# Strassen-type up projection: part sums on VectorE, the MLP's output turned row block by row block, and the gate's norm gain folded into its weights

## The chip, the cores and the metric

The kernel runs on one core of a Trainium2 chip. The metric is the device time of one execution in microseconds (us); less is better. Engines are named as the profile names them: PE is TensorE, DVE is VectorE, ACT is ScalarE, POOL is GpSimd, SP issues the weight loads.

## What is computed

One layer of a hybrid decoder for 512 tokens and a width of 1024, everything in float32. Before the stretch that the change touches lie the input projections, a gated linear recurrence, stick-breaking attention and their merge `m`. The change touches what follows:

```
x = x + merged @ w_out
h2 = rmsnorm(x, norm_mlp_g)
x = x + square(relu(h2 @ w_mlp_up)) @ w_mlp_down      # 1024 -> 4096 -> 1024
h3 = rmsnorm(x, norm_ple_g)
x = x + sigmoid(h3 @ w_ple_gate) * (p @ w_ple)
return rmsnorm(x, norm_final_g)
```

## The kernel before

**Precision and weights.** PE multiplies in fp32r. Each float32 operand is split in a high part, rounded to fp32r by a cast on ACT (L55), and a low part, the difference, formed on DVE (L56); `split_scaled` (L59, L60) does the same for an operand that is to be multiplied by a gain per partition. `prod` (L119 to L124) makes every product of three matmuls: high by high, high by low, low by high. Weights come in halves of 128 partitions by 1024 columns (512 KB): SP loads one into a `raw` buffer (3 of them), ACT and DVE split it into `whi` and `wlo` (3 each). `next_half` hands out the half whose turn it is in the list `halves`, and has the next one loaded and split. The instructions of each engine are put in order by a scheduler at build time, and each engine runs its own list in that order; buffers are given by pools and tags, and a tile that takes the space of an older one waits until that is read out.

**Up projection.** The weight of a group `g` (of 8) consists of four quarters, rows r and columns c. In place of eight products of quarters, seven are made (L623, L625, L626), numbered 1 to 7. Their activations are sums of halves of `x1`, made once during the output projection and kept split in `xa`, `xb`, `xc` (L587 to L604). Their weights are quarters (1: quarter 00, 2: 10, 3: 11) or sums of quarters: 5 is 01 - 00, 7 is 11 - 01, 6 is 11 less the sum of 5, 4 is 10 less the sum of 6. `up_part` (a maker that `next_half` calls) forms a sum in `tw` on POOL (L570) and splits it. `tw` has tag F1, the space of `x1`, which the last additions on DVE (L595, L604) still read. A product is 24 matmuls of 256 columns, a group 168. The order in a group is UP_ORDER, (1, 7, 5, 6, 3, 2, 4). The results are put together in `u` and `w`: u is product 1 plus 6, w is 7 plus 5, then w + u on POOL (L652); `relu2` makes the activation of the next projection on ACT (L634, L635).

**Between.** Blocks of `x1` are turned into rows `x1t` (`to_rows`) as they come. The squares for the norm (`sqm`) follow at once. After the last group, `p` is split into `psp`, whose space is that of `xa`; the small product `p @ w_ple` gives `ple`.

**Down projection.** 32 steps of 24 matmuls of 512 columns go into eight PSUM banks `dn`, in DN_ORDER; each step splits its activation into `ah`, `al` (pool `dnx`) and its weight half. The last three steps go row block by row block, and after each block DVE adds the scaled bank to `x2t` (L716).

**Tail.** When all blocks are through, `x2t` is turned by PE (L725, eight tiles x2T of four 128 by 128 transposes), multiplied by the gain of the norm on DVE (L727, `xg`) and split into `h3` (L728). The gate's weight halves pg0 to pg2 are in the stream of halves; pg3 to pg7 are loaded into `wb3` and `wb1`. The gate product `pgt` runs for all row blocks over the first six of eight parts, then over the last two, then `gate_post`.

Of the kernel before, what the change touches and what calls it, by code (L numbers as in the profile page):

```python
# [27 lines left out]
UP_ORDER = (1, 7, 5, 6, 3, 2, 4)  # L28
DN_ORDER = [h + 2 * g + i for g in range(8) for h in (0, 16) for i in range(2)]
# [5 lines left out]
def hybrid_layer(ctx, tc, xT, pT, vecs, gfin, gates, w_in, w_bl, w_ba, w_out,  # L35
# [202 lines left out]
    with tc.tile_pool(name="st", bufs=1) as st, \  # L238
# [304 lines left out]
    sums = []  # L543
    raws = {}

    def quarter(g, r, c):
# [4 lines left out]
    def up_part(gi, name, kt):

        g, i = gi
        if i == 1:
            src = quarter(g, 0, 0)
        elif i == 2:
            src = quarter(g, 1, 0)
        elif i == 3:
            src = quarter(g, 1, 1)
        else:  # L560
            if not sums:
                sums.append(big.tile([P, 4, 1024], F32, tag="F1", name="tw"))
            tw = sums[0]
            src = tw[:, i - 4]
            a, b = {7: ((1, 1), (0, 1)), 5: ((0, 1), (0, 0)), 6: ((1, 1), None), 4: ((1, 0), None)}[i]
            b = quarter(g, *b) if b else tw[:, 1] if i == 6 else tw[:, 2]
# [8 lines left out]
    makers["up"] = up_part  # L575
    for n in OUT_ORDER:
# [22 lines left out]
        to_rows(x1, x1t, n)  # L599

    ssm = const.tile([P, 2 * NB], F32, name="ssm")
    for tb in range(NB):
        for h in range(2):
            t = tmp_tile(f"sqm{tb}{h}")  # L604
            sc.activation(t, x1t[:, tb, h * 512:(h + 1) * 512], AF.Square,
                          accum_out=ssm[:, 2 * tb + h:2 * tb + h + 1])
    rs2 = const.tile([P, NB], F32, name="rs2")
    ssv = ssm.rearrange("p (t h) -> p t h", h=2)
    ve.tensor_tensor(rs2, ssv[:, :, 0], ssv[:, :, 1], op=ALU.add)
    ve.tensor_scalar(rs2, rs2, 1.0 / D, EPS, op0=ALU.mult, op1=ALU.add)  # L610
    ve.reciprocal(rs2, rs2)


    act = [big.tile([P, 16, 2, H], F32, tag="B1", name="act0"), big2.tile([P, 16, 2, H], F32, tag="B3", name="act1")]
# [20 lines left out]

    for g in range(8):
# [8 lines left out]
        sc.copy(w, by)
        bz = bank(pp, f"upZ{g}")
        products(g, 5, bz, True)
        ve.tensor_tensor(w, bz, w, op=ALU.add)
# [223 lines left out]
```

## Time and profile before

| what | us |
|---|---|
| median of 3 runs | 958.0 |
| the runs | 952.49 to 958.74 |
| the profiled execution | 956.24 |
| its span in the trace | 954.5 |
| PE busy | 923.2 |
| DVE busy | 619.7 |
| ACT busy | 503.3 |
| POOL busy | 174.9 |

The profiled execution lies 1.8 us below the median; 1.7 us of it lie outside its span. A row of the trace that gives one instruction reads: start and duration in us, engine, line, operation, output and inputs, shapes, number of instructions; in brackets, how long the engine had waited and which instruction released it. Durations of matmuls are modelled and overlap; a matmul's cost is read from start to start.

### The profile page before, as it was taken

What the parts mean: (1) busy time and instruction counts of PE and PEld (TensorE: products, weight loads), DVE (VectorE), ACT (ScalarE), POOL (GpSimd) and SP (SyncE); (2) the same over time, 40 slices, a digit from 0 to 9 for tenths busy, and PEclk for the clock granted to TensorE, in tenths of its full rate; (3) what the DMA queues carried; (4) which work ended last, traced back from release to release, by engine and by line L of the source; (5) the groups of instructions that cost most, each with busy time, mean ns of one, the idle gap of its engine ahead of it and who ended that gap; (6) DMA issues with size and microseconds to landing.
All of it is one profiled execution on the core that took longest, in us unless ns stands there. A gap on an engine that the chain in (4) does not pass through costs nothing. (4 is left out here: it accounts for less than half of the span.)

```text
span 954.5 us, 12767 instructions
## 1 busy us (share of the span) xinstructions
PE 923.2 (97%) x4858; PEld 793.9 (83%) x4858; DVE 619.7 (65%) x851; ACT 503.3 (53%) x794; POOL 174.9 (18%) x187
## 2 busy tenths in 40 slices
PE   8989999999999999999999699999999999999896
PEld 7878888888888888888888699999988888888685
DVE  6697766889998985435566677677753333332866
ACT  6455868767777764422244556656554323222633
POOL 0010000133242330000000466666500000000000
PEclk9999999999999999999999799999999999999999
DMA  7232232321212212522321233332243223233302
GB/s 240 93 110 89 67 107 69 111 67 67 67 67 67 67 67 67 198 89 89 111 88 45 76 102 91 114 106 90 89 133 109 90 93 106 89 103 118 111 0 89
DMA packets 25116, 89.46 MB, mean 94 GB/s; under 512 B 2912, under 2 KB 2912, under 8 KB 24800
## 3 DMA queue, kind: packets, MB, share of 16 engines
q1 hardware_dynamic: 24480, 87.61, 28.2%
q10 hardware_dynamic: 576, 1.05, 0.3%
q8 instruction: 38, 0.62, 0.3%
q14 instruction: 22, 0.18, 0.1%
HBM read 86.55 MB, written 2.10 MB: 93 GB/s over the span
## 5 line engine op out<-in xcount | busy, mean ns | idle before, releaser
L123 PE MATMUL dn<-wlo_dn,ah 128*128 128x512 f32 x256 | 99.7, 390 | 0.0
L124 PE MATMUL dn<-whi_dn,al 128*128 128x512 f32 x256 | 98.8, 389 | 0.0
L122 PE MATMUL dn<-whi_dn,ah 128*128 128x512 f32 x256 | 98.0, 390 | 0.0
L56 DVE TENSOR_TENSOR wlo_up<-tw,whi_up 128x1024 fp32r<-128x1024 f32 x32 | 73.0, 2300 | 29.8 <-ACT whi_up L55 29.8
L570 POOL TENSOR_TENSOR tw<-raw_up,raw_up 128x1024 f32<-128x1024 f32 x16 | 45.4, 2840 | 219.5 <-DVE s L595 167.4
L56 DVE TENSOR_TENSOR al<-act,ah 128x512 fp32r<-128x512 f32 x32 | 21.9, 692 | 87.7 <-ACT ah L55 87.7
L55 ACT CAST ah<-act 128x512 fp32r<-128x512 f32 x32 | 19.7, 624 | 104.6 <-PE dn L123 104.6
L160 POOL TENSOR_SCALAR_AFFINE_SELECT r<-r 128x128 f32<-128x128 f32 x64 | 29.9, 467 | 179.1 <-ACT r L428 174.5
L432 DVE TENSOR_TENSOR_SCAN pr<-r,zero 128x128 f32<-128x128 f32 (+1 forms) x64 | 54.2, 847 | 10.6 <-POOL r L160 10.1
L123 PEld LDWEIGHTS dn<-wlo_dn,ah 128*128 128x128 f32 x256 | 48.3, 189 | 10.2
L122 PEld LDWEIGHTS dn<-whi_dn,ah 128*128 128x128 f32 x256 | 48.3, 189 | 10.0
L124 PEld LDWEIGHTS dn<-whi_dn,al 128*128 128x128 f32 x256 | 48.0, 188 | 10.0
L56 DVE TENSOR_TENSOR wlo_dn<-raw_dn,whi_dn 128x1024 fp32r<-128x1024 f32 x32 | 39.2, 1225 | 24.3 <-ACT whi_dn L55 24.3
L570 POOL TENSOR_TENSOR tw<-raw_up,tw 128x1024 f32<-128x1024 f32 x16 | 45.0, 2814 | 2.4 <-DMA raw_up<-in_w_up_dram 1.8
L623 PE MATMUL upY<-xa,whi_up 128*128 128x256 f32 x128 | 37.4, 292 | 6.7 <-ACT whi_up L55 6.7
L55 ACT CAST whi_up<-tw 128x1024 fp32r<-128x1024 f32 x32 | 33.3, 1044 | 19.7 <-PE upX L625 15.0
L428 ACT ACTIVATE r<-z 128x128 f32<-128x128 f32 (+1 forms) x64 | 28.6, 446 | 27.5 <-PE z L424 26.9
L55 ACT CAST whi_up<-raw_up 128x1024 fp32r<-128x1024 f32 x24 | 25.2, 1051 | 31.4 <-PE upZ L625 24.1
L626 PE MATMUL upY<-xa,wlo_up 128*128 128x256 f32 x128 | 38.1, 298 | 2.9 <-DVE wlo_up L56 2.8
L625 PE MATMUL upY<-xa,whi_up 128*128 128x256 f32 x128 | 37.2, 291 | 0.0
L626 PE MATMUL upA<-xa,wlo_up 128*128 128x256 f32 x128 | 36.2, 283 | 0.0
L625 PE MATMUL upA<-xa,whi_up 128*128 128x256 f32 x128 | 36.2, 283 | 0.0
(323 smaller groups left out, 2905.6 us busy)
## 6 DMA issues: line engine op xcount, KB each, us to landing
raw_up<-in_w_up_dram SPq DMA_DIRECT2D x32, 512.0 KB, 3.9
raw_dn<-in_w_dn_dram SPq DMA_DIRECT2D x32, 512.0 KB, 3.3
raw_u<-in_w_in_dram SPq DMA_DIRECT2D x16, 512.0 KB, 3.4
raw_qk<-in_w_in_dram SPq DMA_DIRECT2D x16, 512.0 KB, 3.5
raw_gl<-in_w_in_dram SPq DMA_DIRECT2D x8, 512.0 KB, 3.4
raw_ga<-in_w_in_dram SPq DMA_DIRECT2D x8, 512.0 KB, 3.4
raw_bl<-in_w_bl_dram SPq DMA_DIRECT2D x8, 512.0 KB, 3.4
raw_ba<-in_w_ba_dram SPq DMA_DIRECT2D x8, 512.0 KB, 3.4
```

The costliest lines, as they stand in the source:

```text
L55: sc.copy(hi, src)
L56: ve.tensor_tensor(lo, src, f32(hi), op=ALU.subtract)
L122: pe.matmul(ps, lh, rh, start=(first and i == 0), stop=False)
L123: pe.matmul(ps, lh, rl, start=False, stop=False)
L124: pe.matmul(ps, ll, rh, start=False, stop=(last and i == n - 1))
L160: gp.affine_select(block, block, pattern=[[-1, P]], compare_op=ALU.is_gt, fill=fill, base=0, channel_multiplier=1)
L428: sc.activation(r[:, 0:w], z[:, 0:w], AF.Sigmoid, scale=-0.125)
L432: ve.tensor_tensor_scan(pr[:, 0:w][:, ::-1], r[:, 0:w][:, ::-1], zero.broadcast_to([P, w]), 1.0, op0=ALU.mult, op1=ALU.add)
L570: gp.tensor_tensor(src, quarter(g, *a), b, op=ALU.subtract)
L623: pe.matmul(o, wh[:, k, c], x[:, 0, k, :], start=(first and fi == 0 and k == 0), stop=False, skip_group_check=True)
L625: pe.matmul(o, wh[:, k, c], x[:, 1, k, :], start=False, stop=False, skip_group_check=True)
L626: pe.matmul(o, wl[:, k, c], x[:, 0, k, :], start=False, stop=(k == 3), skip_group_check=True)
```

## The change

**Sums of quarters.** They are made on DVE (`part_sum`) rather than on POOL. Group 0's sums lie in the space of `act0`, which is not written until later; the others lie in `tw`. `up_part` loads a group's quarters in the order 00, 01, 10, 11. w + u moves to DVE too. UP_ORDER is (1, 5, 2, 7, 6, 3, 4). `next_half` builds parts two ahead; `raw`, `whi` and `wlo` still have three buffers each.

**Norm of the MLP's output.** A block of `x1` is turned one block later, the last one behind product 1 of group 0; the squares go to groups 1 to 4; the split of `p` goes ahead of product 4 of the last group, into the space of `xc`.

**Tail.** `x2t` is turned by `turn_rows`, one row block behind the last down products, and split into `h3` straight from PSUM. The gain is folded into the gate's weights (`gate_part`). Of the eight gate halves six are loaded, scaled and split during the down projection and stay resident (`wg`, `wb1`), pg6 and pg7 come through the stream. `ah` and `al` lie in a ring in F1's space; DN_ORDER is range(32).

```diff
-UP_ORDER = (1, 7, 5, 6, 3, 2, 4)
-DN_ORDER = [h + 2 * g + i for g in range(8) for h in (0, 16) for i in range(2)]
+UP_ORDER = (1, 5, 2, 7, 6, 3, 4)
+DN_ORDER = range(32)
...
+        while len(state["ready"]) < state["ahead"] and state["i"] + 1 < len(halves):
+            state["i"] += 1
...
+    def part_sum(g, i, a, b):
+        if g == 0:
+            sums[g, i] = act[0][:, 2 * i:2 * i + 2].rearrange("p f a h -> p (f a h)")
+        else:
+            if g == 1 and i == 5:
+                sums["tw"] = big.tile([P, 4, 1024], F32, tag="F1", name="tw")
+            sums[g, i] = sums["tw"][:, i - 4]
+        ve.tensor_tensor(sums[g, i], a, b, op=ALU.subtract)
...
-            if i == 7:
+            if g == 0:
                 quarter(g, 0, 0)
-                quarter(g, 0, 1)
-            gp.tensor_tensor(src, quarter(g, *a), b, op=ALU.subtract)
+            quarter(g, 0, 1)
+            quarter(g, 1, 0)
+        elif i == 5:
+            part_sum(g, 5, raws[g, 0, 1], raws[g, 0, 0])
+            quarter(g, 1, 1)
+        elif i == 7:
+            part_sum(g, 7, raws[g, 1, 1], raws[g, 0, 1])
+            part_sum(g, 6, raws[g, 1, 1], sums[g, 5])
+            if g < 7:
+                quarter(g + 1, 0, 0)
+        elif i == 6:
+            part_sum(g, 4, raws[g, 1, 0], sums[g, 6])
...
-        gp.tensor_tensor(w, w, u, op=ALU.add)
+        ve.tensor_tensor(w, w, u, op=ALU.add)
...
+        if g == 7:
+            praw = load_raw(pT, "p").rearrange("p (k s) -> p k s", k=2)
+            psp = upx.tile([P, 2, 2, S], F32R, tag="xc", name="psp")
+            split(psp[:, 0], psp[:, 1], praw)
         products(g, 4, by, False)
...
-    psp = big.tile([P, 2, 2, S], F32R, tag="B2", name="psp")
-    split(psp[:, 0], psp[:, 1], praw)
...
+    def gate_part(hi, lo, raw, i):
+        for k in range(2):
+            c = slice(k * 512, (k + 1) * 512)
+            split_scaled(hi[:, c], lo[:, c], raw[:, c], vec("gple", 2 * (i % 4) + k))
...
+        if i in (6, 10):
+            n = i // 4 - 1
+            gate_early(n, wg[:, 2 * n], wg[:, 2 * n + 1])
+        if i in (18, 20, 22, 24):
+            n = i // 2 - 9
+            gate_early(2 + n, wb1[:, 2 * n], wb1[:, 2 * n + 1])
...
-            xg = tmp_tile(f"xg{tb}{h}").rearrange("p (n s) -> p n s", n=4)
-            ve.tensor_tensor(xg, pt, gp3[:, 4 * h:4 * h + 4].unsqueeze(2).broadcast_to([P, 4, P]), op=ALU.mult)
-            split(h3[:, 0, 4 * h:4 * h + 4, t], h3[:, 1, 4 * h:4 * h + 4, t], xg)
+            split(h3[:, 0, 4 * h:4 * h + 4, t], h3[:, 1, 4 * h:4 * h + 4, t], pt)
...
+        if tb > 0:
+            turn_rows(tb - 1)
...
-    for tb in range(NB):
-        gate_rows(rows[tb], tb, range(0, 6))
-    for tb in range(NB):
-        gate_rows(rows[tb], tb, range(6, 8))
+        gate_rows(rows[tb], tb, range(0, KT))
+        if tb == 0:
+            turn_rows(3)
```

What DVE ran in group 1 of the up projection before; the digits behind wlo_up are the group and the product, those behind raw_up the group and the quarter:

```order
L56 TENSOR_TENSOR wlo_up1_7_5137<-tw_4895,whi_up1_7_5136 128x1024
L662 TENSOR_TENSOR c21_0_5123<-upY0_4930,u0_4892 128x512
L56 TENSOR_TENSOR wlo_up1_5_5168<-tw_4895,whi_up1_5_5167 128x1024
L56 TENSOR_TENSOR wlo_up1_6_5199<-tw_4895,whi_up1_6_5198 128x1024
L56 TENSOR_TENSOR wlo_up1_3_5229<-raw_up1_11_5133,whi_up1_3_5228 128x1024
L648 TENSOR_TENSOR w1_5129<-upZ1_5196,w1_5129 128x512
L56 TENSOR_TENSOR wlo_up1_2_5264<-raw_up1_10_5261,whi_up1_2_5263 128x1024
L651 TENSOR_TENSOR u1_5128<-upX1_5227,u1_5128 128x512
```

And the same stretch of DVE's list with the change, where L557 is `part_sum`:

```order
L56 TENSOR_TENSOR wlo_up1_5_5087<-tw_5082,whi_up1_5_5086 128x1024
L667 TENSOR_TENSOR c21_0_5114<-upY0_4981,u0_4877 128x512
L557 TENSOR_TENSOR tw_5082<-raw_up1_11_5084,raw_up1_01_5045 128x1024
L557 TENSOR_TENSOR tw_5082<-raw_up1_11_5084,tw_5082 128x1024
L56 TENSOR_TENSOR wlo_up1_2_5123<-raw_up1_10_5047,whi_up1_2_5122 128x1024
L557 TENSOR_TENSOR tw_5082<-raw_up1_10_5047,tw_5082 128x1024
L56 TENSOR_TENSOR wlo_up1_7_5157<-tw_5082,whi_up1_7_5156 128x1024
L56 TENSOR_TENSOR wlo_up1_6_5187<-tw_5082,whi_up1_6_5186 128x1024
L557 TENSOR_TENSOR tw_5082<-raw_up2_01_5281,raw_up2_00_5154 128x1024
L56 TENSOR_TENSOR wlo_up1_3_5219<-raw_up1_11_5084,whi_up1_3_5218 128x1024
```

The four sums of a group now stand between the low parts, and the sum for the next group's product 5 stands ahead of the low part of product 3; the low parts come in the new order of products.

DVE's list at the end of the output projection, with the change; x1 is the residual that `ps_o3` and `ps_o7` are added to:

```order
L56 TENSOR_TENSOR xc_4483<-s12_6_4756,xc_4483 128x256
L557 TENSOR_TENSOR act0_4485<-raw_up0_11_4826,raw_up0_01_4777 128x1024
L557 TENSOR_TENSOR act0_4485<-raw_up0_11_4826,act0_4485 128x1024
L587 TENSOR_TENSOR x1_3938<-x1_3938,ps_o3_4774 128x512
L56 TENSOR_TENSOR wlo_up0_5_4829<-act0_4485,whi_up0_5_4828 128x1024
```

Two sums of group 0 now stand ahead of the addition of `ps_o3` in DVE's list; before, no sum stood on DVE.

PE's list at the end of the down projection, before, and below it with the change; dn30 and dn31 are the banks of the last row block, x2T the turned tiles, pgt0 the first gate product:

```order
L122 MATMUL dn31_6866<-whi_dn31_7869,ah31_7873 128x512
L123 MATMUL dn31_6866<-wlo_dn31_7870,ah31_7873 128x512
L124 MATMUL dn31_6866<-whi_dn31_7869,al31_7874 128x512
L725 MATMUL x2T00_7981<-ident_82,x1t_4484 128x128 x4
L725 MATMUL x2T01_7990<-ident_82,x1t_4484 128x128 x4
L725 MATMUL x2T10_7999<-ident_82,x1t_4484 128x128 x4
L725 MATMUL x2T11_8008<-ident_82,x1t_4484 128x128 x4
L725 MATMUL x2T20_8017<-ident_82,x1t_4484 128x128 x4
L122 MATMUL pgt0_0_8109<-whi_pg0_0_7879,h3_7883 128x512
```

```order
L124 MATMUL dn21_6871<-whi_dn31_7844,ring_6865 128x512
L122 MATMUL dn30_6872<-whi_dn29_7780,ring_6865 128x512
L757 MATMUL x2T00_7918<-ident_82,x1t_4484 128x128 x4
L757 MATMUL x2T01_7925<-ident_82,x1t_4484 128x128 x4
L757 MATMUL x2T10_7956<-ident_82,x1t_4484 128x128 x4
L757 MATMUL x2T11_7963<-ident_82,x1t_4484 128x128 x4
...
L124 MATMUL dn31_6873<-whi_dn31_7844,ring_6865 128x512
L757 MATMUL x2T20_7994<-ident_82,x1t_4484 128x128 x4
L757 MATMUL x2T21_8001<-ident_82,x1t_4484 128x128 x4
L122 MATMUL pgt0_0_8015<-wg_6874,h3_7868 128x512
```

The tiles of row blocks 0 and 1 now stand ahead of the last row block's down products rather than behind them; block 2 stands ahead of the gate.

## Rows read from the trace of the kernel before

**Rows 1.** The page's first part: busy time, share of the span, instructions.

```profile
PE 923.2 (97%) x4858; PEld 793.9 (83%) x4858; DVE 619.7 (65%) x851; ACT 503.3 (53%) x794; POOL 174.9 (18%) x187
```

**Rows 2.** Windows: stretch and length; busy PE, PEld, DVE, ACT, POOL; clock; DMA share; GB/s.

```profile
527.00:542.00 15.00, 6.88 (x32) 6.37 (x31) 9.44 (x9) 9.41 (x22) 10.15 (x4) 0.66 0.22 72
560.00:703.00 143.00, 140.01 (x1141) 137.37 (x1141) 106.58 (x76) 86.07 (x117) 84.01 (x32) 1.00 0.33 100
703.00:709.00 6.00, 4.00 (x12) 3.01 (x11) 5.36 (x7) 5.13 (x8) 0.00 (x0) 0.72 0.63 203
709.00:890.00 181.00, 181.00 (x800) 149.83 (x800) 61.63 (x66) 56.16 (x80) 0.00 (x0) 1.00 0.29 95
```

**Rows 3.** Timeline of PE, start of the up projection and its second group.

```profile
526.62 0.60 PE L526 MATMUL xT<-ident,x 128*128 128x128 f32 x4
...
533.93 0.58 PE L623 MATMUL upY<-xa,whi_up 128*128 128x256 f32 x1 [6.71 <-ACT whi_up L55]
...
536.13 0.58 PE L626 MATMUL upY<-xa,wlo_up 128*128 128x256 f32 x1 [1.41 <-DVE wlo_up L56]
...
555.68 0.28 PE L623 MATMUL upA<-xa,whi_up 128*128 128x256 f32 x1
```

**Rows 4.** Timeline of POOL and DVE at the same place.

```profile
527.71 4.84 POOL L570 TENSOR_TENSOR tw<-raw_up,raw_up 128x1024 f32<-128x1024 f32 x2 [167.41 <-DVE s L595]
532.63 2.37 POOL L570 TENSOR_TENSOR tw<-raw_up,tw 128x1024 f32<-128x1024 f32 x1
536.26 1.22 DVE L56 TENSOR_TENSOR wlo_up<-tw,whi_up 128x1024 fp32r<-128x1024 f32 x1
```

**Rows 5.** Timeline of PE: a wait in group 2, the start of group 7, its end.

```profile
579.24 0.28 PE L623 MATMUL upY<-xa,whi_up 128*128 128x256 f32 x1
579.36 0.28 PE L625 MATMUL upY<-xa,whi_up 128*128 128x256 f32 x1
579.90 0.39 PE L626 MATMUL upY<-xa,wlo_up 128*128 128x256 f32 x1 [0.27 <-DVE wlo_up L56]
...
682.01 0.28 PE L623 MATMUL upA<-xa,whi_up 128*128 128x256 f32 x1
...
703.01 0.28 PE L626 MATMUL upY<-xa,wlo_up 128*128 128x256 f32 x1
```

**Rows 6.** Groups by form, 560 to 700 us: busy us, mean ns; idle before, releasers.

```profile
L56 DVE TENSOR_TENSOR wlo_up<-tw,whi_up 128x1024 fp32r<-128x1024 f32 x27 | 61.5, 2299 | 22.5 <-ACT whi_up L55 22.5
L570 POOL TENSOR_TENSOR tw<-raw_up,raw_up 128x1024 f32<-128x1024 f32 x12 | 34.8, 2898 | 44.6 <-DMA raw_up<-in_w_up_dram 44.6
L56 DVE TENSOR_TENSOR wlo_up<-raw_up,whi_up 128x1024 fp32r<-128x1024 f32 x20 | 27.3, 1367 | 1.4 <-ACT whi_up L55 1.4
L651 DVE TENSOR_TENSOR u<-upX,u 128x512 f32<-128x512 f32 x7 | 4.8, 692 | 4.9 <-PE upX L626 4.9
```

**Rows 7.** The same groups, 709 to 890 us: the down projection, POOL idle.

```profile
L56 DVE TENSOR_TENSOR wlo_dn<-raw_dn,whi_dn 128x1024 fp32r<-128x1024 f32 x31 | 38.0, 1225 | 24.0 <-ACT whi_dn L55 24.0
```

**Rows 8.** Tile raw_up: time of its loads.

```profile
DMA to landing us min/median/max: 3.6/3.9/4.9
```

**Rows 9.** Timeline of ACT and PE between up and down projection.

```profile
704.20 1.04 ACT L55 CAST psp<-raw_p 128x1024 fp32r<-128x1024 f32 x1
...
705.29 0.62 PE L122 MATMUL ple<-whi_ple,psp 128*128 128x512 f32 x1 [2.00 <-ACT psp L55]
...
709.04 0.39 PE L123 MATMUL dn<-wlo_dn,ah 128*128 128x512 f32 x1
```

**Rows 10.** Timeline of PE between down projection and gate.

```profile
891.76 0.39 PE L124 MATMUL dn<-whi_dn,al 128*128 128x512 f32 x1
...
896.12 1.71 PE L725 MATMUL x2T<-ident,x1t 128*128 128x128 f32 x8 [2.66 <-DVE xg L727]
...
901.37 0.50 PE L122 MATMUL pgt<-whi_pg,h 128*128 128x512 f32 x1 [1.83 <-ACT h L55]
```

More of the change, by code (lines that the diff above doesn't have):

```diff
@@ L540, in put @@
         split(left[i][:, 0, k, :], left[i][:, 1, k, :], src)
-    sums = []
+    act = [big.tile([P, 16, 2, H], F32, tag="B1", name="act0")]
     raws = {}
+    sums = {}
     def quarter(g, r, c):
-        if (g, r, c) not in raws:
-            raws[g, r, c] = load_raw(w_up[g][:, (2 * r + c) * 1024:(2 * r + c + 1) * 1024], f"up{g}_{r}{c}")
-        return raws[g, r, c]
+        raws[g, r, c] = load_raw(w_up[g][:, (2 * r + c) * 1024:(2 * r + c + 1) * 1024], f"up{g}_{r}{c}")
+    def part_sum(g, i, a, b):
[6 more added lines that the diff above has]
+        ve.tensor_tensor(sums[g, i], a, b, op=ALU.subtract)
     def up_part(gi, name, kt):
@@ L554, in up_part @@
         if i == 1:
[L555 to L566, printed above, removed]
-            if i == 7:
-                quarter(g, 0, 0)
-                quarter(g, 0, 1)
-            gp.tensor_tensor(src, quarter(g, *a), b, op=ALU.subtract)
+            if g == 0:
+                quarter(g, 0, 0)
+            quarter(g, 0, 1)
[10 more added lines that the diff above has]
+            part_sum(g, 4, raws[g, 1, 0], sums[g, 6])
+        src = raws[g, 0 if i == 1 else 1, 1 if i == 3 else 0] if i < 4 else sums[g, i]
         hi, lo = w_tiles(name)
@@ L575, in hybrid_layer @@
     makers["up"] = up_part
+    state["ahead"] = 2
+    turn = None
     for n in OUT_ORDER:
@@ L598, in hybrid_layer @@
                          x1[:, n, :].rearrange("p (a h) -> p a h", a=2), g)
-        to_rows(x1, x1t, n)
-    ssm = const.tile([P, 2 * NB], F32, name="ssm")
-    for tb in range(NB):
[L603 to L614, printed above, removed]
+        if turn is not None:
+            to_rows(x1, x1t, turn)
+        turn = n
+    act.append(big2.tile([P, 16, 2, H], F32, tag="B3", name="act1"))
     def products(g, i, bank, first):
@@ L634, in relu2 @@
         sc.activation(dst, t, AF.Square)
+    ssm = const.tile([P, 2 * NB], F32, name="ssm")
     for g in range(8):
@@ L642, in hybrid_layer @@
         sc.copy(u, ba)
+        if g == 0:
+            to_rows(x1, x1t, turn)
+        bz = bank(pp, f"upZ{g}")
+        products(g, 5, bz, True)
+        sc.copy(w, bz)
+        products(g, 2, ba, False)
+        relu2(act[0][:, f, 0, :], ba, f"r11_{g}")
         by = bank(pq, f"upY{g}")
         products(g, 7, by, True)
[L645 to L648, printed above, removed]
+        ve.tensor_tensor(w, by, w, op=ALU.add)
         bx = bank(pp, f"upX{g}")
@@ L679, in hybrid_layer @@
             sc.copy(ple[:, tb, c], ps)
-    dnx = ctx.enter_context(tc.tile_pool(name="dnx", bufs=4))
+    up.close()
+    gw = ctx.enter_context(tc.tile_pool(name="gw", bufs=1))
+    ring = big.tile([P, 4, 2, S], F32R, tag="F1", name="ring")
     x2t = x1t
@@ L712, in hybrid_layer @@
             down(i, ops, (tb,))
-        t = slice(tb * P, (tb + 1) * P)
         for h in range(2):
```

74 lines of the change are left out of this document (42 added, 32 removed).

## The prediction

> **What bounds the kernel now.** I read the page's first part, then windows, then timelines of PE where a window shows a gap, then the other engines at those places. PE is busy for 923.2 of 954.5 us, 97% [rows 1]; a change to the other engines can win only where PE waits or runs at its lower clock. The windows say where [rows 2]. In the down projection PE issues 800 matmuls in 181.00 us, 0.226 us for one of 512 columns, without a gap. In the loop of the up projection it is busy 140.0 of 143 us. At the start of that stage it is busy 6.88 of 15 us at a mean granted clock of 0.66, so part of it at 1.2 rather than 2.4 GHz; between up and down projection 4.00 of 6 us, clock 0.72. A fourth gap, between down projection and gate, comes last below.
>
> Start of the up stage [rows 3]: PE has nothing after the transposes at 526.62, waits 6.71 us for `whi_up` and 1.41 us for `wlo_up`. The cause is on POOL [rows 4]: its sum had waited 167.41 us, until DVE's line 595 gave `x1` free, for `tw` has the space of `x1`; then sums of some 2.4 us follow one another. In the loop two matmuls start 0.12 us apart, and the third, which needs `wlo_up`, 0.54 us after the second [rows 5]: POOL's sum, ACT's cast and DVE's low part of product 7 come just in time or too late. DVE's low part costs 2.30 us with `tw`, 1.37 us with a raw quarter [rows 6]. The same shape costs 1.225 us in the down projection, where POOL is idle [rows 7], and 1.22 us with `tw` itself at 536.26, between two sums [rows 4]. So I read the 2.30 us as a cost of running beside POOL.
>
> **The time that can be won.** Each gap is time from start to start less the matmuls in it, at 0.12 us for 256 columns, 0.226 us for 512, and 0.11 us for a transpose (my estimate, just under the 0.12 us of a matmul of 256 columns).
>
> - A, start: 526.62 to 555.68 is 29.06 us; four transposes and six products of 24 need 0.44 + 17.28 = 17.72. Excess 11.3 us, of it 8.1 the two waits and the rest mostly the low clock.
> - B, loop: product 1 starts at 555.68 and, six groups on, at 682.01 [rows 3, 5]. That is 126.33 us for 6 x 168 x 0.12 = 120.96, 0.9 us a group. The last group takes 21.12 us to 703.13 against 20.16. Excess 6.3 us over seven groups.
> - C, between [rows 9]: PE is through at 703.13 and starts at 705.29, after a wait for ACT's `psp`, 2.16 us; nine matmuls then take 3.75 us instead of 2.03. Excess 3.9 us.
> - D, before the gate [rows 10]: the last down product ends at 891.99, the gate starts at 901.37, 9.38 us; 24 transposes and two matmuls need 3.09. Excess 6.3 us, with waits of 2.66 and 1.83 us in it.
>
> Together 27.8 us. Everything else PE does is the same before and after: the same products, as many transposes.
>
> **The change, part by part.** *A.* Group 0's sums go into `act0`'s space and need no `x1`; they can run during the output projection. The wait on POOL goes. What is late next: DVE. Two sums (2 x 1.22 to 1.37 us) stand ahead of the addition of the output products `ps_o3` in DVE's list, and the first of them waits for quarter 11. Behind it are queued the additions of `ps_o3` and `ps_o7` and the splits of the last activations, for which products 1 and 5 wait. Nothing lost if the quarter has landed and product 1 (2.9 us) covers the delay; two sums and a load, 2 x 1.37 + 4.9 = 7.6 us, if nothing does (the load's longest time is 4.9 [rows 8]). PE's own work between covers most of it: I take 0.8 us, no wait long enough for the clock, which stayed at 1.00 through the loop's waits of some 0.3 us [rows 2, 5].
>
> *B.* POOL leaves the loop; 32 sums and 8 additions go to DVE. Per group DVE then has 7 low parts and 4 sums of 1024 columns and 5 operations of 512. With the durations of rows 6 and 7: 11 x 1.225 + 5 x 0.69 = 16.9 us of 20.16. Before it was 4 x 2.30 + 3 x 1.37 and four of the short ones. The sums stand one or two products ahead of their use, and product 2, a bare quarter, between 5 and 7 gives product 7 another 2.9 us. By hand from these durations, product 7's high part is there some 0.75 us before PE wants it, its low part and the others 1.5 us or more. The tightest load is quarter 11 of the next group: asked for about 17 us into a group, landed 3.9 us later [rows 8], when its sum is due at 21; a load of 5.5 us would still do. I take 0.2 us left of 6.3; the bounds are none and 6.3.
>
> Here a rule speaks to the price. The Trainium skill, SBUF - State Buffer, section Who interferes with whom, says that VectorE and GpSimd share a pair of ports as an exclusive lock, so that a DVE operation with two SBUF inputs and a POOL operation block each other. By it the low parts fall to 1.22 us as soon as POOL is gone, and the sum stands; rows 4, 6 and 7 agree (1.22 and 1.225 against 2.30). If the operands were the reason instead, the sum would be that of the slower rival below.
>
> *C.* `psp` moves into the space of `xc`, free when product 3 of the last group is done, so its cast (1.04 us [rows 9]) runs beside product 4's 2.9 us. ACT has the squares of the last group in its list too. I leave 0.3 us for `psp` and 0.6 us for the first `whi_dn` behind it; bounds none and 3.9.
>
> *D.* Row blocks 0 and 1 are turned ahead of the last block's 18 down products (4.1 us), block 2 ahead of the gate, block 3 behind the gate's first 24 matmuls (5.4 us). Eight multiplications by the gain go from DVE. The gate's splits, now with the gain, run during the down projection: six halves, each with 1024 columns on ACT and on DVE, in a window where DVE is busy 62 and ACT 56 of 181 us [rows 2]. At 2 x 0.75 us (two half-width pieces, an estimate from 1.37 and 0.69 us of rows 6) that is 9 us on DVE, hidden; were it not, 9 us would be the price. SP's six loads (512 KB each) share the three raw buffers with the stream, of which one step needs a new one every 24 x 0.226 = 5.4 us; the DMA share there is 0.29. I take 0.2 us left; bounds none and one wait of 2.7.
>
> **Sum.** Left over: 0.8 + 0.2 + 0.9 + 0.2 = 2.1 us. Saved: 27.8 - 2.1 = 25.7 us. From the profiled execution's 956.24 us that is 930.5. The median of the runs is 1.8 us above that execution, the fastest run 3.8 us below it; I forecast 931.0 us.
>
> **Rivals.**
> 1. *The start still waits.* DVE stands still for quarter 11, PE waits several us at product 1 or 5 and drops to 1.2 GHz as before. For it: SP's loads go in order, and DVE's list puts the sum ahead of activations. Against: PE still has transposes and product 1. Price some 5 us: 936.
> 2. *The load chain is late in the loop.* Quarter 11 lands late, product 7's high part is late, and PE's list has two matmuls of product 7 ahead of product 2. Some 1 us in seven groups: 938. Against: the longest load is 4.9 us.
> 3. *No lead.* Parts are built two ahead, but `whi` and `wlo` keep three buffers: a part cannot be written until the product three before it is through, in either kernel. Then the loop keeps its 0.9 us per group: 937. Against: what was late there was the sum and the slow low part, and both move.
> 4. *Slower: DVE becomes the bound of the loop.* If the 2.30 us belong to the operands in `tw` and the sums cost as much, DVE has 8 x 2.30 + 3 x 1.22 + 5 x 0.69 = 25.5 us a group, 5.35 over PE's 20.16. Seven groups: +37.5 in place of 6.3, with A, C and D still saving 19.6 us: 956.2 + 31.2 - 19.6 = 968. It begins to decide when the mean wide operation takes over (20.16 - 3.45) / 11 = 1.52 us. Against: the 1.22 us at 536.26, with `tw` and POOL between sums. The Trainium skill, Perfetto Trace Analysis, section Optimizing Scalar/DVE Operations, says that where DVE is saturated, work may be moved to other engines, GPSIMD among them; the change goes the other way. By that advice DVE, at 106.6 of 143 us [rows 2], is the engine not to load.
>
> **How the numbers follow.** Forecast 0.66, rival 1 0.13, rival 2 0.10, rival 3 0.05, rival 4 0.06. A measurement of this kernel can tell about 1%, 9.6 us. Forecast and rivals 1 to 3 lie below 948.4: 0.94; of these 0.05 go to "same" for two of them together and for a rival 4 by halves (wide operations of about 1.9 us). So faster 0.89, same 0.05, slower 0.06. Range: the forecast's own goes from 928.4 (nothing left over) less some 3 us of spread, 925, to 934; with rivals 1 to 3, alone or two at a time, 945.
>
> **What would show it.** Right: no PE wait over 1 us between 520 us and the end of the up stage; product 1 to product 1 in 20.2 us; `wlo_up` and the sums near 1.22 us; DVE near 17 of 20 us in the loop; a granted clock of 1.00 there, between the projections and at the gate; the gate starting within 4 us of the last down product. Wrong: `wlo_up` above 1.5 us; PE's waits in the loop on DVE; a clock below 0.9 at the start; a wait for `whi_dn` or the gate's halves during the down projection.

## The result, and the profile after

The changed kernel takes 929.28 us (median of 4 runs, 928.57 to 929.90), the kernel before 956.22 us (median of 4, 952.49 to 958.74): a ratio of 0.9721, 95% interval 0.9684 to 0.9759, so 2.8% faster. The forecast was 931.0. The span of the profiled execution falls from 954.5 to 927.6 us, by 26.9.

The page's first part after, which answers to [rows 1], and PE's line and clock line of its second part:

```profile
PE 914.0 (99%) x4858; PEld 790.3 (85%) x4858; DVE 620.7 (67%) x891; ACT 505.8 (55%) x802; POOL 67.5 (7%) x147
...
PE   9989999999999999999999999999999999999996
...
PEclk9999999999999999999999999999999999999998
```

PE has the same 4858 instructions. Its share goes from 97 to 99%, the clock line has no dip in the stages that were touched, and POOL falls from 174.9 to 67.5 us. DVE took the sums over and is no busier, 620.7 against 619.7 us: its other operations became shorter by about as much as it received.

The windows of the same stages after, which answer to [rows 2] (stretch and length; busy PE, PEld, DVE, ACT, POOL; clock; DMA share; GB/s):

```profile
523.30:546.00 22.70, 22.70 (x191) 22.66 (x191) 17.69 (x25) 16.24 (x24) 0.00 (x0) 1.00 0.24 71
546.00:683.00 137.00, 137.00 (x1144) 137.00 (x1143) 110.87 (x113) 92.31 (x134) 0.00 (x0) 1.00 0.36 105
683.00:690.00 7.00, 6.78 (x39) 5.63 (x39) 6.48 (x9) 6.46 (x10) 0.00 (x0) 1.00 0.48 165
690.00:868.00 178.00, 178.00 (x790) 147.55 (x789) 69.50 (x77) 62.00 (x89) 0.00 (x0) 1.00 0.36 115
868.00:880.00 12.00, 12.00 (x67) 10.26 (x66) 9.80 (x25) 7.55 (x19) 0.00 (x0) 1.00 0.01 2
```

From the start of the up stage to the gate PE is never idle but for 0.22 us between the projections, all at a clock of 1.00. To compare kernels I add up, for each of the four gaps of the prediction, the time from each PE start to the next less 0.226, 0.12 or 0.11 us for 512, 256 or 128 columns; this takes in both waits and time at the low clock. A ends and B begins at about 555 us, where group 1 begins in the kernel before; in the kernels that are earlier by then the first half of group 1 counts in A. Before: A (start) 11.35, B (loop) 6.33, C (between) 3.92, D (before the gate) 6.50 us. After: 0.0, 0.0, 0.72 and 0.11. Together they fall by 27.3 us, where the span lost 26.9; the other 0.4 us lie behind PE's last matmul (8.8 us before, 9.2 after).

The price of DVE's work in the loop after, groups by form from 560 to 690 us (busy us, mean ns; idle before, releasers), which answer to [rows 6]:

```profile
L56 DVE TENSOR_TENSOR wlo_up<-tw,whi_up 128x1024 fp32r<-128x1024 f32 x24 | 29.4, 1224 | 4.5 <-ACT whi_up L55 4.5
L56 DVE TENSOR_TENSOR wlo_up<-raw_up,whi_up 128x1024 fp32r<-128x1024 f32 x18 | 21.9, 1219 | 1.9 <-ACT whi_up L55 1.9
...
L557 DVE TENSOR_TENSOR tw<-raw_up,tw 128x1024 f32<-128x1024 f32 x12 | 14.6, 1219 | 0.0
...
L557 DVE TENSOR_TENSOR tw<-raw_up,raw_up 128x1024 f32<-128x1024 f32 x11 | 13.5, 1223 | 7.2 <-DMA raw_up<-in_w_up_dram 7.1
```

Low parts from `tw` fall from 2.30 to 1.22 us, those from raw quarters from 1.37 to 1.22, and a sum costs the same 1.22 us where it cost POOL 2.90.

DVE's timeline at the end of the output projection after shows the place where the forecast feared for the start:

```profile
518.01 1.23 DVE L557 TENSOR_TENSOR act<-raw_up,raw_up 128x1024 f32<-128x1024 f32 x1 [0.98 <-DMA raw_up<-in_w_up_dram]
519.15 1.22 DVE L557 TENSOR_TENSOR act<-raw_up,act 128x1024 f32<-128x1024 f32 x1
520.28 0.68 DVE L587 TENSOR_TENSOR x<-x,ps_o 128x512 f32<-128x512 f32 x1
```

DVE does stand still for quarter 11, but for 0.98 us, and PE has work until the activations are there. PE's timeline before the gate, which answers to [rows 10]:

```profile
872.66 0.40 PE L124 MATMUL dn<-whi_dn,ring 128*128 128x512 f32 x1
872.90 1.04 PE L757 MATMUL x2T<-ident,x1t 128*128 128x128 f32 x8
873.69 0.47 PE L122 MATMUL pgt<-wg,h 128*128 128x512 f32 x1
```

The gate starts 0.8 us after the last down product's matmul ends at 872.89; eight transposes fill that time.

### The profile page after: what moved, and what is told of

It is laid out like the page before. It is cut to its first block, busy times and chain, and to the rows that moved or that the text cites. A ratio compares the mean times of both kernels' runs of the same rounds, so it can differ in the third digit from the quotient of the medians.

```text
span 927.6 us, 12721 instructions
## 1 busy us (share of the span) xinstructions
PE 914.0 (99%) x4858; PEld 790.3 (85%) x4858; DVE 620.7 (67%) x891; ACT 505.8 (55%) x802; POOL 67.5 (7%) x147
## 5 line engine op out<-in xcount | busy, mean ns | idle before, releaser
L123 PE MATMUL dn<-wlo_dn,ring 128*128 128x512 f32 x256 | 99.6, 390 | 0.0
L124 PE MATMUL dn<-whi_dn,ring 128*128 128x512 f32 x256 | 99.5, 389 | 0.0
L122 PE MATMUL dn<-whi_dn,ring 128*128 128x512 f32 x256 | 97.4, 390 | 0.2 <-ACT whi_dn L55 0.2
L56 DVE TENSOR_TENSOR ring<-act,ring 128x512 fp32r<-128x512 f32 x32 | 22.0, 691 | 79.8 <-ACT ring L55 79.8
L55 ACT CAST ring<-act 128x512 fp32r<-128x512 f32 x32 | 19.6, 623 | 97.1 <-PE dn L123 97.1
L122 PEld LDWEIGHTS dn<-whi_dn,ring 128*128 128x128 f32 x256 | 48.0, 188 | 10.5 <-ACT whi_dn L55 0.5
L123 PEld LDWEIGHTS dn<-wlo_dn,ring 128*128 128x128 f32 x256 | 48.1, 188 | 10.0
L124 PEld LDWEIGHTS dn<-whi_dn,ring 128*128 128x128 f32 x256 | 48.1, 188 | 9.8
L56 DVE TENSOR_TENSOR wlo_up<-tw,whi_up 128x1024 fp32r<-128x1024 f32 x28 | 34.2, 1224 | 4.8 <-ACT whi_up L55 4.8
L55 ACT CAST whi_up<-tw 128x1024 fp32r<-128x1024 f32 x28 | 29.3, 1046 | 14.8 <-PE upZ L623 8.1
L621 PE MATMUL upA<-xa,whi_up 128*128 128x256 f32 x128 | 36.3, 284 | 0.0
L623 PE MATMUL upA<-xa,whi_up 128*128 128x256 f32 x128 | 36.3, 283 | 0.0
L55 ACT CAST whi_dn<-raw_dn 128x1024 fp32r<-128x1024 f32 x32 | 33.5, 1046 | 4.9 <-PE dn L124 4.1
```

Source lines behind the costliest of these rows:

```text
L55: sc.copy(hi, src)
L56: ve.tensor_tensor(lo, src, f32(hi), op=ALU.subtract)
L122: pe.matmul(ps, lh, rh, start=(first and i == 0), stop=False)
L123: pe.matmul(ps, lh, rl, start=False, stop=False)
L124: pe.matmul(ps, ll, rh, start=False, stop=(last and i == n - 1))
L621: pe.matmul(o, wh[:, k, c], x[:, 0, k, :], start=(first and fi == 0 and k == 0), stop=False, skip_group_check=True)
```

## The experiments

Twelve kernels ran, in three rounds of four in the order below. Each round has its own runs of the kernel before, and the ratios are to these (medians 954.65, 954.21 and 955.74 us). The changed kernel has many parts in each gap, so most runs undo one part. The theory: POOL beside DVE is the cause in the loop, the place of group 0's sums at the start, the place of `psp` between the projections, and the early turning with the resident weights before the gate. The rivals stand with each run.

**Group 0's sums back in the space of x1.**

```diff
-        if g == 0:
-            sums[g, i] = act[0][:, 2 * i:2 * i + 2].rearrange("p f a h -> p (f a h)")
-        else:
-            if g == 1 and i == 5:
-                sums["tw"] = big.tile([P, 4, 1024], F32, tag="F1", name="tw")
-            sums[g, i] = sums["tw"][:, i - 4]
+        if g == 0 and i == 5:
+            sums["tw"] = big.tile([P, 4, 1024], F32, tag="F1", name="tw")
+        sums[g, i] = sums["tw"][:, i - 4]
```

> Group 0's sums lie in tw again, in the space of x1; all else as in the changed kernel (929.3 us). Theory (the place of group 0's sums is what ended the 6.7 us wait): DVE's first sum stands behind its last read of x1, so product 5 waits for a sum of 1.22, a cast of 1.04 and a low part of 1.22 us, some 3 us behind the end of product 1; 932 to 935 us, more if the clock falls. Rival (DVE's quicker sums ended it, wherever they lie): within 1 us of 929.3.

Measured: 934.17 us, ratio to before 0.9771 (0.9748 to 0.9793). Gap A is 4.98 us, the others as in the changed kernel. PE's waits at the start in that run:

```profile
529.51 0.39 PE L618 MATMUL upZ<-xb,whi_up 128*128 128x256 f32 x1 [2.39 <-ACT whi_up L55]
...
530.46 0.39 PE L618 MATMUL upA<-xa,whi_up 128*128 128x256 f32 x1 [0.45 <-ACT whi_up L55]
```

The theory's size came out. So of A's 11.35 us some 5 hang on the place of the sums alone, with the sums on DVE.

**The sums of groups 1 to 7 back on POOL.**

```diff
-        ve.tensor_tensor(sums[g, i], a, b, op=ALU.subtract)
+        (ve if g == 0 else gp).tensor_tensor(sums[g, i], a, b, op=ALU.subtract)
```

> The sums of groups 1 to 7 go back to POOL, order and lead as in the changed kernel. Theory (the 2.3 us low parts come from POOL beside DVE, and the order 1, 5, 2, 7 with its lead hides most of it): wlo_up from tw back at 2.0 us or more, but PE loses less than 0.3 us a group; 929.5 to 931.5 us. Rival (POOL beside DVE is itself what cost the loop 0.9 us a group): 934 to 936 us. A third reading (the 2.3 us belong to the operands, not to POOL) is already against the changed kernel's 1.22 us; it would show wlo_up unchanged at 1.22.

Measured: 933.31 us, ratio 0.9766 (0.9743 to 0.9789), 3.6 to 3.9 us over the next two kernels of the same round, which keep the sums on DVE. Gap B is 3.93 us, and 0.36 us more lie in the first half of group 1. The groups by form from 545 to 690 us:

```profile
L56 DVE TENSOR_TENSOR wlo_up<-tw,whi_up 128x1024 fp32r<-128x1024 f32 x27 | 55.5, 2057 | 24.2 <-ACT whi_up L55 17.2 <-PE upZ L623 6.8
L557 POOL TENSOR_TENSOR tw<-raw_up,tw 128x1024 f32<-128x1024 f32 x14 | 38.8, 2768 | 0.5
```

The low parts are at 2.06 us again: it was POOL, not the tile. But the theory's other half, that order and lead hide it, failed: the loop lost 3.9 us. 1.39 us of it are one gap, and its cause stands in DVE's list. Line 677 (the small operation of the norm, 128 by 4) in the run with POOL's sums, with POOL's timeline at that time, and below them the same line in the changed kernel (operation: min/median/max in ns, first and last start):

```profile
L677 DVE TENSOR_SCALAR rs<-rs x1: 2330/2330/2330, 631.2 to 631.2; 128x4 f32<-128x4 f32 x1
```

```profile
631.07 4.88 POOL L557 TENSOR_TENSOR tw<-raw_up,tw 128x1024 f32<-128x1024 f32 x2
```

```profile
L677 DVE TENSOR_SCALAR rs<-rs x1: 163/163/163, 631.6 to 631.6; 128x4 f32<-128x4 f32 x1
```

Four columns took 2.33 us instead of 0.16 while a sum was running on POOL, and the low part behind them was late for PE.

**psp split behind the last group again.**

```diff
-        if g == 7:
-            praw = load_raw(pT, "p").rearrange("p (k s) -> p k s", k=2)
-            psp = upx.tile([P, 2, 2, S], F32R, tag="xc", name="psp")
-            split(psp[:, 0], psp[:, 1], praw)
         products(g, 4, by, False)
...
+    praw = load_raw(pT, "p").rearrange("p (k s) -> p k s", k=2)
+    psp = big.tile([P, 2, 2, S], F32R, tag="B2", name="psp")
+    split(psp[:, 0], psp[:, 1], praw)
     w = next_pair("ple")
```

> psp is split behind the last group's products again, in the space of xa. Theory: PE waits 2 us between the projections and runs some matmuls at 1.2 GHz as before; 3 us more than the changed kernel, 932 to 933 us. Rival (the wait is hidden by what PE can draw forward from the down projection): within 0.5 us of 929.3.

Measured: 929.40 us, ratio 0.9721 (0.9698 to 0.9744): no difference that the times show, though gap C is 1.50 us against 0.72. The theory (3 us more) fell. The time is the rival's, but not for its reason, for PE does wait. PE's wait in that run, and ACT's list at the place:

```profile
686.54 0.50 PE L122 MATMUL ple<-whi_ple,psp 128*128 128x512 f32 x1 [1.14 <-ACT psp L55]
```

```profile
685.44 1.04 ACT L55 CAST psp<-raw_p 128x1024 fp32r<-128x1024 f32 x1
686.39 1.04 ACT L55 CAST whi_dn<-raw_dn 128x1024 fp32r<-128x1024 f32 x1
```

PE waits for the one cast. In the kernel before, ACT cast the first `whi_dn` ahead of `psp` (at 704.20 [rows 9]), and PE waited 2.00 us:

```profile
703.25 1.05 ACT L55 CAST whi_dn<-raw_dn 128x1024 fp32r<-128x1024 f32 x1 [0.70 <-PE upY L625]
```

Here `psp` comes first. The clock stays at 2.4 GHz: it is 1.00 over 685 to 693 us.

**All rows turned behind the last down product.**

```diff
-        if tb > 0:
-            turn_rows(tb - 1)
+    for tb in range(NB):
+        turn_rows(tb)
...
-            turn_rows(3)
```

> All four row blocks are turned behind the last down product; the gain stays folded and the gate's halves stay resident. Theory (early turning is half of the gain before the gate, the shorter chain from PSUM to h3 and the resident weights the other half): the gate starts 2 to 3 us later than the work needs, 931.5 to 932.5 us. Rival A (the fold and the resident weights alone did it): within 0.5 us of 929.3. Rival B (the early turning alone did it): the whole 6 us come back, 935 us.

Measured: 929.72 us, ratio 0.9726 (0.9700 to 0.9751). Rival A holds: gap D is 0.22 us. PE's timeline:

```profile
871.24 0.39 PE L124 MATMUL dn<-whi_dn,ring 128*128 128x512 f32 x1
871.47 3.22 PE L757 MATMUL x2T<-ident,x1t 128*128 128x128 f32 x28
874.51 0.50 PE L122 MATMUL pgt<-wg,h 128*128 128x512 f32 x1
```

Twenty-eight transposes run without a wait, and by their end the part of `h3` that the gate's first product needs is there.

**The old order of products, sums on DVE.** The quarters are loaded to suit (00, 01, 11, 10).

```diff
-UP_ORDER = (1, 5, 2, 7, 6, 3, 4)
+UP_ORDER = (1, 7, 5, 6, 3, 2, 4)
...
```

> The changed kernel with the products of a group in the old order 1, 7, 5, 6, 3, 2, 4, and the quarters loaded to suit. Theory (DVE's quicker sums and low parts have lead enough in either order): PE loses under 0.2 us a group, 929 to 931 us. Rival (product 2 between 5 and 7 is what hides product 7's chain): the 0.9 us a group come back, 934 to 936 us.

Measured: 928.55 us, ratio 0.9722 (0.9693 to 0.9751); gap B 0.21 us. The theory holds; the order is worth nothing once the sums are on DVE.

**One part ahead.**

```diff
-    state["ahead"] = 2
```

> The changed kernel with weight parts built one product ahead in place of two; buffers are three in both. Theory (three buffers set the lead, not the list): within 1 us of 929.3. Rival (the lead in the list counts, since each engine runs its list in order and sums would stand behind the waits of the product before): 0.3 us or more a group, 932 us or more.

Measured: 929.00 us, ratio 0.9726 (0.9702 to 0.9751); gap B 0.0. The theory holds: the lead in the list is worth nothing either. Here is ACT's cast of the same part in the changed kernel, and below it in this run:

```profile
610.68 1.05 ACT L55 CAST whi_up<-tw 128x1024 fp32r<-128x1024 f32 x1 [1.02 <-PE upZ L623]
```

```profile
610.58 1.05 ACT L55 CAST whi_up<-tw 128x1024 fp32r<-128x1024 f32 x1 [1.01 <-PE upZ L622]
```

In both the cast waits 1.0 us for PE to be through with an earlier product, so the buffers and not the list set when it runs.

**The kernel before, with group 0's sums in act0's space.**

```diff
+    act = [big.tile([P, 16, 2, H], F32, tag="B1", name="act0")]
...
-            if not sums:
-                sums.append(big.tile([P, 4, 1024], F32, tag="F1", name="tw"))
-            tw = sums[0]
+            if g == 0:
+                tw = act[0][:, 8:16].rearrange("p (i f) a h -> p i (f a h)", i=4)
+            else:
+                if not sums:
+                    sums.append(big.tile([P, 4, 1024], F32, tag="F1", name="tw"))
+                tw = sums[0]
...
```

> The kernel before with one thing changed: group 0's sums lie in act0's space; they stay on POOL. Theory: the 6.7 us wait and the low clock at the start go, POOL's sums run during the output projection, at most 1.5 us of the 11.3 are left; loop and tail as before: 945 to 948 us against 956. Rival (POOL's slow sums would come too late anyway): 950 us or more.

Measured: 949.42 us, ratio 0.9934 (0.9911 to 0.9957), between the two expectations. The long wait is gone, and gap A falls from 11.35 to 2.4 us, with 1.1 us more just ahead of it; B and C are as before; D is 7.7 us, 1.2 more than before, though nothing in that stage was changed. The rest of A is POOL's: with the sums of group 1 it is late at 548 us.

**The kernel before, with the sums and w + u on DVE.**

```diff
-            gp.tensor_tensor(src, quarter(g, *a), b, op=ALU.subtract)
+            ve.tensor_tensor(src, quarter(g, *a), b, op=ALU.subtract)
...
-        gp.tensor_tensor(w, w, u, op=ALU.add)
+        ve.tensor_tensor(w, w, u, op=ALU.add)
```

> The kernel before with one thing changed: the sums and w + u are on DVE; their place, the order and the lead are the old ones. Theory (POOL beside DVE and its 2.4 to 2.9 us sums are most of the loop's 0.9 us a group): wlo_up from tw at 1.22 us, the loop's waits nearly gone (5 to 6 us), the start still waits for x1 but 2 to 3 us less: 947 to 950 us. Rival (the order and lead are what the loop lacked): the loop keeps its 0.9 us a group, 953 to 954 us.

Measured: 946.02 us, ratio 0.9908 (0.9881 to 0.9936), 1 us under the theory's range. The windows of the loop and of gap C in that run:

```profile
560.00:691.00 131.00, 131.00 (x1094) 131.00 (x1093) 102.91 (x104) 82.92 (x112) 0.00 (x0) 1.00 0.36 109
691.00:699.00 8.00, 6.03 (x31) 4.97 (x30) 5.82 (x8) 5.54 (x10) 0.00 (x0) 1.00 0.61 194
```

The low parts take 1.22 us (groups by form, 560 to 691 us):

```profile
L56 DVE TENSOR_TENSOR wlo_up<-tw,whi_up 128x1024 fp32r<-128x1024 f32 x25 | 30.5, 1220 | 3.7 <-ACT whi_up L55 3.7
```

PE is busy for every one of 131 us: gap B goes from 6.33 to 0.0 by this alone, with the old order and the old lead. DVE's busy share rises only from 75 [rows 2] to 79%. C falls to 2.30 us, since the clock stays at 1.00 there. D is 7.6 us, again over 1 us more than before. A falls to 7.56; the two waits of [rows 3] are shorter, but there:

```profile
529.86 0.58 PE L623 MATMUL upY<-xa,whi_up 128*128 128x256 f32 x1 [3.80 <-ACT whi_up L55]
...
531.43 0.58 PE L626 MATMUL upY<-xa,wlo_up 128*128 128x256 f32 x1 [0.78 <-DVE wlo_up L56]
```

**Four parts undone together.** old_order, one_ahead, psp_late and turn_late in one kernel.

> Four parts of the change undone together, each of which alone had cost 0.5 us or less in the earlier runs: old order of products, one part ahead, psp behind the last group, all rows turned behind the last down product. Left of the change are the sums on DVE, group 0's in act0's space, the folded gain and the resident gate halves (with the ring, the order of the down steps and the later squares). Theory (these carry the whole gain, and the other parts only spare 0.8 us of wait at psp): 929 to 931 us. Rival (the four cover for one another): 933 us or more.

Measured: 929.65 us, ratio 0.9734 (0.9708 to 0.9760). The theory holds: gaps 0.0, 0.19, 1.35 and 0.23 us. These four parts of the change carry nothing that the times show.

**Turned late, gain on the rows.** On top of turn_late; the gate's halves stay resident, unscaled.

```diff
-            split_scaled(hi[:, c], lo[:, c], raw[:, c], vec("gple", 2 * (i % 4) + k))
+            split(hi[:, c], lo[:, c], raw[:, c])
...
-            split(h3[:, 0, 4 * h:4 * h + 4, t], h3[:, 1, 4 * h:4 * h + 4, t], pt)
+            xg = tmp_tile(f"xg{tb}{h}").rearrange("p (n s) -> p n s", n=4)
+            ve.tensor_tensor(xg, pt, gp3[:, 4 * h:4 * h + 4].unsqueeze(2).broadcast_to([P, 4, P]), op=ALU.mult)
+            split(h3[:, 0, 4 * h:4 * h + 4, t], h3[:, 1, 4 * h:4 * h + 4, t], xg)
```

> As turn_late (929.7 us), and the gain multiplies the turned rows on DVE again; the gate's halves, not scaled, stay resident. Theory (the halves' casts and loads stood in the way before the gate, not the gain): 929.5 to 931 us, at most one wait of 1 us. Rival (the eight multiplications in the chain from PSUM to h3 made the waits): 932 to 935 us.

Measured: 930.61 us, ratio 0.9740 (0.9721 to 0.9760); gap D 0.88 us. The theory holds. PE turns seven tiles without a wait, the eighth waits for the gain's multiplication:

```profile
871.80 3.22 PE L759 MATMUL x2T<-ident,x1t 128*128 128x128 f32 x28
875.18 0.66 PE L759 MATMUL x2T<-ident,x1t 128*128 128x128 f32 x4 [0.16 <-DVE xg L762]
```

The kernel before turns its tiles into one pool of three PSUM banks, and it is its fourth tile that waits 2.66 us for the same multiplication [rows 10]. The changed kernel uses a second pool of four, and this run keeps it.

**Turned late, gate halves late.** On top of turn_late; three scaled halves in the stream, five loaded behind the rows.

```diff
...
-        if i in (6, 10):
-            n = i // 4 - 1
-            gate_early(n, wg[:, 2 * n], wg[:, 2 * n + 1])
-        if i == 17:
-            wb1 = big.tile([P, 8, 1024], F32R, tag="B1", name="wb1")
-        if i in (18, 20, 22, 24):
-            n = i // 2 - 9
-            gate_early(2 + n, wb1[:, 2 * n], wb1[:, 2 * n + 1])
...
+    wq[0] = [next_half(f"pg{j}") for j in range(3)]
+    wb1 = big.tile([P, 8, 1024], F32R, tag="B1", name="wb1")
+    gate_early(3, wb3[:, 0], wb3[:, 1])
+    for j in range(4):
+        gate_early(4 + j, wb1[:, 2 * j], wb1[:, 2 * j + 1])
...
-        gate_rows(rows[tb], tb, range(0, KT))
+        gate_rows(rows[tb], tb, range(0, 6))
+    for tb in range(NB):
+        gate_rows(rows[tb], tb, range(6, 8))
```

> As turn_late (929.7 us), but the gate's halves come as in the kernel before: three in the stream, five loaded behind the turned rows, the gate product over six parts and then two; the gain stays folded. Theory (the halves' casts and low parts in ACT's and DVE's lists ahead of h3, one of them behind a load, made the waits): PE waits 2 us or more between down projection and gate, 932 to 936 us. Rival (they are hidden, and the gain's multiplication was it): 929.5 to 931 us.

Measured: 930.55 us, ratio 0.9745 (0.9722 to 0.9768); gap D 1.54 us. PE and ACT before the gate in that run:

```profile
874.23 0.50 PE L122 MATMUL pgt<-whi_pg,h 128*128 128x512 f32 x1 [1.15 <-DVE h L56]
```

```profile
867.45 3.95 ACT L59 ACTIVATE whi_pg<-raw_pg,vt 128x512 fp32r<-128x512 f32 x6
871.30 0.56 ACT L55 CAST h<-x2T 128x512 fp32r<-128x512 f32 x1
```

The scaled casts of the gate's halves hold ACT until 871.3, and `h3` is late, but by one wait of 1.15 us rather than the 2.66 and 1.83 of [rows 10]. The theory (2 us or more) fell; the time is the rival's, whose reason, the gain's multiplication, the run before does not bear out. Neither undoing brings D's 6.5 us back; each brings some 1 us, close to what the times can tell.

**Idle work on POOL beside the loop.** The changed kernel with eight operations per group whose result nothing reads.

```diff
...
         ve.tensor_tensor(w, w, u, op=ALU.add)
+        for j in range(8):
+            gp.tensor_tensor(scr, u, u, op=ALU.subtract)
```

> The changed kernel with eight operations of 512 columns per group added on POOL, which nothing waits for (they read u and write a scratch tile). Theory (DVE operations with two SBUF inputs stretch beside POOL, whatever their tile): POOL is busy some 9 us a group, the 11 wide DVE operations average 1.5 us or more, DVE comes close to PE's 20.16 us and PE loses 0 to 1 us a group, 929 to 937 us. Rival (only an operation that shares a tile with POOL's is stretched): wide operations stay at 1.22 us, and so does the time.

Measured: 952.75 us, ratio 0.9976 (0.9960 to 0.9992): nine tenths of the gain are gone. The groups by form from 560 to 700 us:

```profile
L658 POOL TENSOR_TENSOR scr<-u 128x512 f32<-128x512 f32 x49 | 83.7, 1707 | 64.3 <-DVE u L655 61.0
L56 DVE TENSOR_TENSOR wlo_up<-tw,whi_up 128x1024 fp32r<-128x1024 f32 x25 | 34.8, 1408 | 0.3 <-ACT whi_up L55 0.3
L56 DVE TENSOR_TENSOR wlo_up<-raw_up,whi_up 128x1024 fp32r<-128x1024 f32 x19 | 33.3, 1751 | 1.8 <-ACT whi_up L55 1.8
...
L557 DVE TENSOR_TENSOR tw<-raw_up,tw 128x1024 f32<-128x1024 f32 x12 | 23.9, 1988 | 0.0
L557 DVE TENSOR_TENSOR tw<-raw_up,raw_up 128x1024 f32<-128x1024 f32 x11 | 14.3, 1300 | 11.8 <-DMA raw_up<-in_w_up_dram 11.8
```

POOL shares no written tile with these operations, and they stretch all the same, to a mean of 106.3 / 67 = 1.59 us. What PE waited for from 560 to 720 us (us in total, times, longest):

```profile
PE upA L624 <- DVE wlo_up L56: 6.9, 6, 1.8
PE upY L624 <- DVE wlo_up L56: 3.4, 4, 0.9
```

DVE is now the bound of the loop; no engine's wait in it ends on POOL. Gap B is 16.8 us, more than the theory's top, and 2.1 us more lie in the first half of group 1. Most of it is waits, and some 2.6 us are matmuls at the low clock behind two waits of 2 us (below). Gap C is 7.4 us, with two waits of PE for DVE, 2.0 and 2.1 us, and the low clock behind them. Gaps A to D together account for the 25.4 us by which the span is longer than the changed kernel's. The kernel before lost only 6.3 us in its loop with POOL as busy (84.0 us of 143 [rows 2]): there DVE did not carry the sums.

## Why the prediction was right, and where its reasons were not

The sum was right, by its terms. Saved were to be 25.7 us, the span lost 26.9. Left over were to be 0.8, 0.2, 0.9 and 0.2 us in A to D; left are 0.0, 0.0, 0.72 and 0.11. The term that was most off was the start: I let DVE's wait for quarter 11 reach PE with 0.8 us; DVE waited 0.98 us and PE's own work covered it.

The price that bore the most weight, "11 x 1.225 + 5 x 0.69", came out, at 1.22 us for all four kinds of wide operation. The reading of the 2.30 us as a cost of running beside POOL is shown by three runs: it goes with POOL's sums from the old kernel (1.22 us), comes back with them in the new one (2.06 us), and comes back with POOL work that shares no written tile (1.30 to 1.99 us). The rule of the Trainium skill (SBUF - State Buffer, Who interferes with whom), that the two engines lock each other out of a shared pair of ports, fits these numbers.

The trace of the kernel before shows more than the prediction read from it. From 545 to 704 us, the 29 wide operations of DVE that began while POOL was at work took 1.71 to 3.03 us; the other 24 took 1.21 to 1.23. Additions of 512 columns with one input in PSUM were not stretched: the 14 that began while POOL was at work took 0.68 us. POOL and DVE in group 2:

```profile
576.36 5.75 POOL L570 TENSOR_TENSOR tw<-raw_up,tw 128x1024 f32<-128x1024 f32 x2
...
577.52 2.33 DVE L56 TENSOR_TENSOR wlo_up<-tw,whi_up 128x1024 fp32r<-128x1024 f32 x1 [3.38 <-ACT whi_up L55]
579.77 0.68 DVE L662 TENSOR_TENSOR c<-upY,u 128x512 f32<-128x512 f32 x1
```

So 2.30 us is a mean that depends on when an operation begins. The low part at 536.26, which the prediction placed between two sums, overlapped the second: POOL began it at 536.76 and took 2.94 us, while DVE's operation, begun first, kept its 1.22.

The slower rival's point of decision, a mean wide operation of 1.52 us, was passed in the last run at 1.59 us; DVE became the bound there, with a loss of 18.9 us over seven groups where the bare sum 11 x 1.59 + 5 x 0.69 = 20.9 us, 0.8 us a group over PE's, says 5.5. The sum left out that DVE stood still 11.8 us for quarters, and that PE's clock fell twice: DVE, which runs its list in order, was the bound at 88% busy (123.8 of 140 us).

Three reasons that the prediction gave for its terms failed, though the terms held.
- B: "product 2, a bare quarter, between 5 and 7 gives product 7 another 2.9 us". The old order loses 0.21 us in the loop, one part ahead nothing, and the kernel before loses nothing with the sums on DVE. Rival 3 (no lead) was right in its reason and wrong in its result: the buffers do set when a part is built (ACT's casts above), and no lead is needed.
- C: `psp` moved "so its cast (1.04 us [rows 9]) runs beside product 4's 2.9 us". That part saves 0.8 us of gap and nothing that the times show. With it undone alone, C's other 2.4 us are two things: `psp` ahead of `whi_dn` in ACT's list (a wait of 1.14 in place of 2.00 us), and the low clock that does not come. The order of the two casts is not needed either: in the run with four parts undone ACT casts `whi_dn` first again, PE has down products ahead of `ple` and waits 1.02 us for `whi_dn`, and C is 1.35 us. Which part of the change moved these places in the lists was not tried.
- D: rows turned ahead of the last block's products. Turned late, the gate loses 0.1 us more. What of the 6.5 us each other part carries stays open: gain on rows costs 0.7 us and late halves 1.3 us over turn_late, each alone. Both undone at once was not tried, nor was the second pool of PSUM banks by itself. The wait of 2.66 us [rows 10] points to that pool, which the prediction did not name: the kernel before waits at its fourth tile, the kernels with seven banks at none of the first seven.

How the gain divides, by the two runs that start from the kernel before: the sums on DVE alone save 0.9% (0.6 to 1.2), group 0's place alone 0.7% (0.4 to 0.9), of 2.8% in all. For the rest no run starts from the kernel before; most of it is D, which neither of the two runs shortens. The later squares, the ring and the order of the down steps were never undone.

So the forecast was right in its time and in its main mechanism, POOL beside DVE and the place of group 0's sums. That it was right in C and D too says little for the reasons given there.

## What to carry to other kernels

Where an elementwise operation on DVE has two lengths in one trace, look at what POOL is doing when the long ones begin, before blaming the tile or the order: moving POOL's work to the busier DVE closed the gaps of this loop, since DVE's other operations became shorter by about as much as it took over. Undo the parts of a bundled change one by one and then together: four parts of this one that looked reasoned carry nothing that the times show. A list that runs in order should be judged by its waits, not by its busy share.

## What was not expected of the hardware

A wait of the same length had two prices. Between the projections PE waits 2.00, 1.96 and 1.97 us in the kernel before, with group 0's sums moved, and with the sums on DVE. In the first two its matmuls behind the wait then run at 1.2 GHz for some time (mean clock 0.72 over 6 us [rows 2], 0.79 over 8 us); in the third the clock stays at 1.00. The first two kernels' loops had two waits of some 0.4 us in every group until then, the third's had none. In the window of the second:

```profile
693.00:701.00 8.00, 6.04 (x24) 4.80 (x23) 5.84 (x8) 5.41 (x9) 0.00 (x0) 0.79 0.61 198
```

Gap C is 3.92 and 3.90 us in these two, 2.30 us in the third. That the small waits were part of why is not shown, and two traces speak against it. With POOL's idle work the loop has two waits of about 1 us in a group and a clock of 1.00 there; the clock fell only behind waits of some 2 us:

```profile
574.50:579.00 4.50, 4.44 (x24) 4.45 (x25) 4.50 (x4) 0.39 (x1) 2.80 (x2) 0.62 0.29 65
...
618.00:640.00 22.00, 20.30 (x167) 19.89 (x167) 20.05 (x17) 14.02 (x21) 13.71 (x9) 1.00 0.31 91
```

And in the third kernel the clock fell before the gate (0.82 over 876 to 895 us), behind a wait of 2.7 us and with no wait in the whole down projection. Why a wait of 2 us cost 1.6 us more in two kernels and not in the third stays open.
